# Two-layer decoder step on one core: layer A's y split where it is made, and its transposes moved half a tile back

## The chip, the core and the metric

The kernel runs on one core of a Trainium2 chip. The metric is the device time of one execution in microseconds, as a median over runs. Engines are named as in the trace: PE is TensorE's products, PEld its weight loads, DVE is VectorE, ACT is ScalarE, POOL is GpSimd, and SP is SyncE, whose queue issues the transfers.

## The reference

What is computed, cut to the parts that matter here; D_MODEL is 1024, there are 1024 prompt tokens and 8 x 8 sample tokens, so 1088 rows in all:

```
def short_conv_mixer(u, buf, w_in, w_conv, w_out):        # layer A
    b_gate, c_gate, h, z = split(u @ w_in)
    y, new_buf = causal_dwconv(c_gate * h, buf, w_conv)
    return (b_gate * y * silu(z)) @ w_out, new_buf

def trunk(x, c, ...):
    cs = silu(c)
    for l in range(2):
        shift, scale, gate = split(cs @ w_mod[l] + b_mod[l])
        u = x * (1.0 + scale) + shift
        out = short_conv_mixer(u, ...) if l == 0 else gdn_mixer(u, ...)
        x = layer_norm(ALPHA * x + gate * out, ln_g[l], ln_b[l])
    return x, ...
```

gdn_mixer, layer B, projects u to q, k, v, z and two gate columns for each of 8 heads, convolves, runs a gated delta rule in chunks, norms and projects out.

## The kernel before

Every product is made of three: an operand is split into a high part (a copy rounded to fp32r, on ACT) and a low part (the rest, a subtraction on DVE), and high x high, low x high and high x low are added up in PSUM. The helper split(hi, lo, src) issues the two.

Layer A runs over 8 channel blocks of 128 (chan_a). Each makes four projections of all 1088 tokens, a convolution, and y = b x conv x silu(z), whose last factor POOL multiplies in; y is then stored as fp32 to d_y[0][j]. After the last block comes the out-projection, out_proj(0, ...), over 9 tiles of rows: eight of 128 prompt tokens and tile 8, the 64 samples. For each tile t:

- load_y fetches the tile's y in two halves of four 128-row blocks into a raw buffer and splits it into the parts yh and yl (named wh and wl in the trace). There are three buffers for parts, and one or two for raw data: wts.second lends the second.
- mm(t, hf) does the products of a half: 24 of 512 columns. Tile 8 goes over three column groups instead (512, 256, 256: LAST).
- norm(t) adds the residual x (the tile xt) on DVE, takes the statistics (BN_STATS, BN_AGGR), gets the root from ACT (rt), and computes rs and nm, the scale and bias of the normed tile, in five steps of 128x1.
- finish_a normalizes xt on ACT (xt<-xt,nm,rs). POOL multiplies and adds ln_g and ln_b into x1, which has one buffer and is stored to d_x1. PE transposes the normed tile in eight 128x128 blocks into two PSUM buffers of pt (the trace has t<-cons,xt); below, T0 to T8 are these blocks. ACT applies layer B's modulation (uf, four instructions for each half) and splits it into uh (ACT) and ul (DVE): the operands of layer B's projections.

Behind tile 8, beside_a loads the gate columns (wba) and runs the gate units 0 and 1 (16 products each); gate unit 2 is the first work of gates() in layer B, and needs T8. Layer B's order is written by a planner: streams (chains) and projections (fillers) are taken in the order of times that the class Clock reckons while the program is written. At its start it takes the first step of the chain of gates, and then goes by these times. The order on each engine is what results from the program's order and from the framework's own scheduling; it is fixed before the run.

Of the kernel before, what the change touches and what calls it, by code (L numbers as in the profile page):

```python
# [73 lines left out]
class Clock:  # L74
    """Estimates (in us) of when the queue of an engine gets through what was put into it, and of when tiles are ready;
    they only decide in which order independent work is put into the queues."""

    ready = {}
    # per engine: fixed price, price of an element, from the end until others see the result
# [31 lines left out]
class Weights:  # L111
    """A pool for weight tiles: a buffer for them as loaded (a second one from elsewhere while there is room), buffers for their parts."""
# [18 lines left out]
def tile_trunk(ctx, tc, I, O):  # L131
# [6 lines left out]
    # ------------------------------------------------------------ pools that live throughout  # L138
# [26 lines left out]
    d_y = [dram.tile([KT, P, NT], F32, name=f"d_y{l}") for l in range(2)]  # L165
# [16 lines left out]
    # layer A's prompt shift is kept out of the last group's columns and sits in two columns of its own behind them  # L182
# [7 lines left out]
    def load_half(pool, src, out):  # L190
        """Half of the rows of a weight tile, in two parts; the parts go to out."""
# [53 lines left out]
    def out_proj(l, wk, pairs, wo, gP, gS, finish, ln_in=None, beside=None, constants=None):  # L245
# [14 lines left out]
        def load_y(t, hf):  # L260
            n, o = rows(t)
            yr = wts.raw()
            yh, yl = wts.part()
            SY.dma_start(yr[:, :, :n], d_y[l][4 * hf:4 * hf + 4, :, o:o + n].rearrange("k p t -> p k t"))
            split(yh[:, :, :n], yl[:, :, :n], yr[:, :, :n])
            ys[t, hf] = yh, yl

        def mm(t, hf, cs=(slice(0, 512), slice(512, D))):
            n, o = rows(t)
            if t not in pss:  # L270
                p0, p1 = pair(pairs[t % len(pairs)])
                pss[t] = {0: p0, 512: p1}
                if t == KT:
                    pss[t][768] = bank(0)
# [10 lines left out]
        def norm(t):  # L285
# [4 lines left out]
            cs = (slice(0, 512), slice(512, D)) if t < KT else LAST  # L290
# [21 lines left out]
            return finish(t, n, o, xt, rs, nm, mv[:, 0:1])  # L312
# [11 lines left out]
        else:  # L324
# [5 lines left out]
            load_x(1)  # L330
        wts.second = wk
        stores = []
        for t in range(3, 9):
# [4 lines left out]
            if l and t == 3:  # L338
                for i in EARLY[3]:
                    constants(i) if i < 6 else load_x(i - 6)  # L340
            if t == 3:
                stores.append(norm(0))
            if l:
                load_x(t)
            while stores and t > 3:
                stores.pop(0)()
            stores.append(norm(t - 2))
            if not l:
                load_x(t - 1)
# [9 lines left out]
        if not l:  # L359
            load_x(8)  # L360
            beside()
        stores.append(norm(8))
# [1155 lines left out]
```

## Time and profile before

| | us |
|---|---|
| median of 3 runs | 1397.69 |
| lowest and highest run | 1396.69, 1399.59 |
| span of the profiled execution | 1398.3 |
| layer A, projections | 0 to 430 |
| layer A, out-projection, norm, transposes | 430 to 560 |
| layer B, projections and chunks | 560 to 1290 |
| layer B, out-projection | 1290 to 1398 |

The profiled execution's own time is its span, 1398.3 us; it lies within the runs' range, 0.6 above the median. The bounds of the stages are read off the timeline. A row of the timeline gives start and length in us from the span's start, the engine, the operation with output and inputs, and, in brackets, how long the engine had been idle and which engine, tile or transfer released it. The program's tensors go by their names, t and s and g and o being PSUM tiles.

### The profile page before, as it was taken

The page shows a single profiled execution, that of the slowest core. Times are in us where ns is not written, and L with a number is a line of the kernel's source. Part 1 is how long each engine was busy: PE and PEld are TensorE (multiplying, and loading weights), DVE is VectorE, ACT ScalarE, POOL GpSimd, SP SyncE. Part 2 cuts the span into 40 slices and gives each one's busy share as a digit, 9 for nine tenths or more (in the row PEclk, how much of TensorE's full clock was granted, in tenths as well). Part 3 has the DMA queues.
Part 4 walks back from the last instruction along what each step waited for, and adds up shares of the span by engine and source line. Part 5 has one row for each costly group of instructions (what it writes and reads, how often), then busy time and mean ns, then how long its engine had stood idle before and what let it go on. Part 6 is the DMA issues. An engine that isn't in the chain of part 4 may idle for free.

```text
span 1398.3 us, 27695 instructions
## 1 busy us (share of the span) xinstructions
PE 1325.5 (95%) x10631; PEld 1197.4 (86%) x10631; DVE 907.6 (65%) x2326; ACT 590.8 (42%) x1672; POOL 275.6 (20%) x381
## 2 busy tenths in 40 slices
PE   7999999999999998989999999989999999999897
PEld 5888899999998776988998888988888889887675
DVE  3443234324423988777677988887887887657697
ACT  3421212222111554676656565565555554443221
POOL 0000000000000434112212223231222322221231
PEclk9999999999999999999999999999999999999999
DMA  9735442222213332472121142212222233335862
GB/s 323 246 133 222 163 153 73 72 85 84 68 52 119 121 99 85 152 244 77 32 72 57 50 117 59 87 50 64 74 71 76 75 109 95 115 111 183 241 200 75
DMA packets 119024, 160.23 MB, mean 115 GB/s; under 512 B 21220, under 2 KB 74220, under 8 KB 116844
## 3 DMA queue, kind: packets, MB, share of 16 engines
q1 hardware_dynamic: 118892, 158.46, 35.2%
q8 instruction: 83, 1.36, 0.4%
q14 instruction: 49, 0.40, 0.1%
HBM read 123.61 MB, written 34.82 MB: 113 GB/s over the span
## 4 chain that ended last, share of the span: by engine, by line
PE 33%; DVE 16%; DMA 5%; ACT 4%; issue 2%; POOL 0%; SPq 0%; POOLq 0%; DVEq 0%; ACTq 0%
PE g L106 17%; PE t L106 10%; PE s L106 4%; DVE acc L106 2%; PE o L106 2%; DVE wl L106 2%; DMA wr<-in_wb_dram 1%; ACT junk L106 1%; DMA S<-in_s_dram 1%; DMA rb<-d_rows 1%; DVE EH L106 1%; DVE xt L106 1%; DVE AH L106 1%; DVE YH L106 1%; DVE rk2t L106 1%
## 5 line engine op out<-in xcount | busy, mean ns | idle before, releaser
L106 PE MATMUL g<-uh,wh 128*128 128x384 f32 (+3 forms) x1080 | 381.3, 357 | 3.0 <-ACT xb L106 2.2
L106 PE MATMUL g<-ul,wh 128*128 128x384 f32 (+3 forms) x1080 | 359.9, 336 | 0.0
L106 PE MATMUL g<-uh,wl 128*128 128x384 f32 (+2 forms) x1064 | 356.0, 338 | 0.5 <-DVE wl L106 0.5
L106 DVE TENSOR_TENSOR wl<-wr,wh 128x256 fp32r<-128x256 f32 (+1 forms) x225 | 138.6, 631 | 169.1 <-ACT wh L106 168.7
L106 PEld LDWEIGHTS g<-uh,wh 128*128 128x128 f32 (+1 forms) x1080 | 203.6, 189 | 8.0 <-ACT xb L106 2.7
L106 ACT ACTIVATE wh<-wr 128x256 fp32r<-128x256 f32 (+2 forms) x227 | 108.8, 500 | 236.9 <-PE t L106 117.4
L106 PEld LDWEIGHTS g<-ul,wh 128*128 128x128 f32 (+1 forms) x1080 | 203.7, 189 | 3.3 <-DVE Rs L106 0.2
L106 PEld LDWEIGHTS g<-uh,wl 128*128 128x128 f32 x1064 | 200.9, 189 | 3.8 <-DVE wl L106 1.4
L106 PE MATMUL t<-uh,wh 128*128 128x384 f32 (+3 forms) x540 | 177.2, 336 | 4.6 <-ACT uh L106 3.3
L106 PE MATMUL t<-ul,wh 128*128 128x384 f32 (+3 forms) x540 | 176.3, 334 | 0.1
L106 PE MATMUL t<-uh,wl 128*128 128x384 f32 (+2 forms) x532 | 173.3, 333 | 0.4 <-DVE ve L106 0.4
L106 DVE SCALAR_TENSOR_TENSOR acc<-xb,wbc,acc 128x512 f32<-128x512 f32 (+1 forms) x144 | 118.1, 821 | 10.0 <-ACT acc L106 9.3
L106 PEld LDWEIGHTS t<-uh,wh 128*128 128x128 f32 (+1 forms) x540 | 101.3, 188 | 16.8 <-issue 6.3
L106 PEld LDWEIGHTS t<-ul,wh 128*128 128x128 f32 (+1 forms) x540 | 101.6, 188 | 5.4 <-issue 2.3
L106 PEld LDWEIGHTS t<-uh,wl 128*128 128x128 f32 x532 | 100.2, 189 | 4.0 <-DVE ve L106 0.8
L106 ACT ACTIVATE EH<-t 128x256 f16<-128x256 f32 (+1 forms) x176 | 55.2, 367 | 36.9 <-PE t L106 36.6
L106 ACT ACTIVATE DH<-t 128x256 f16<-128x256 f32 (+1 forms) x128 | 45.8, 383 | 57.6 <-PE t L106 56.8
L106 ACT ACTIVATE xb<-g 128x384 f32<-128x384 f32 (+4 forms) x122 | 48.2, 413 | 37.9 <-PE g L106 36.5
L106 DVE TENSOR_TENSOR YH<-Y,YH 128x256 f16<-128x256 f32 (+1 forms) x104 | 49.5, 479 | 16.8 <-ACT YH L106 16.5
L106 PE MATMUL t<-DH,AH 128*128 128x64 f16 x1176 | 53.5, 193 | 4.1 <-POOL AH L106 1.8
L106 PEld LDWEIGHTS <-AH 128*128 128x128 f16 x1176 | 43.2, 98 | 15.2 <-issue 10.0
L106 PEld LDWEIGHTS <-EH 128*128 128x128 f16 x1120 | 42.7, 98 | 14.5 <-issue 7.6
(367 smaller groups left out, 2432.3 us busy)
## 6 DMA issues: line engine op xcount, KB each, us to landing
wm<-in_wm_dram SPq DMA_DIRECT2D x16, 1024.0 KB
wr<-in_wb_dram SPq DMA_DIRECT2D x64, 256.0 KB
wr<-in_wa_dram SPq DMA_DIRECT2D x62, 256.0 KB
wm<-in_wm_dram SPq DMA_DIRECT2D x16, 512.0 KB
wr<-d_y SPq DMA_DIRECT2D x32, 256.0 KB
S<-in_s_dram SPq DMA_DIRECT2D x32, 256.0 KB
d_y<-cs SPq DMA_DIRECT2D x8, 544.0 KB
wr<-in_wo_dram SPq DMA_DIRECT2D x16, 256.0 KB
```

Source lines behind the costliest of these rows:

```text
L106: return call(*args, **kw)
```

## The change

In chan_a, y is split right after it is complete: the high part into the tile of xb, the low one over sz, and two transfers store them to d_yh and d_yl. load_y of layer A then has two transfers straight into the parts, no raw tile and no split. In out_proj of layer A, norm(t) no longer ends in the transposes: it normalizes, and returns a function that does the rest. That function is called behind the first half of the next tile's products but one (T1 behind all of tile 3's, T6 behind all of tile 8's, T7 and T8 behind the gate units). Tile 8 goes over two groups of 512 columns. gates() gives way once before gate unit 2, until uh[2] and ul[2] are expected. Layer B's out-projection keeps its code. Comments that the change drops aren't shown.

```diff
-    d_y = [dram.tile([KT, P, NT], F32, name=f"d_y{l}") for l in range(2)]
+    d_y = dram.tile([KT, P, NT], F32, name="d_y")
+    d_yh = dram.tile([KT, P, NT], F32, name="d_yh")
+    d_yl = dram.tile([KT, P, NT], F32, name="d_yl")
...
         def load_y(t, hf):
             n, o = rows(t)
-            yr = wts.raw()
-            yh, yl = wts.part()
-            SY.dma_start(yr[:, :, :n], d_y[l][4 * hf:4 * hf + 4, :, o:o + n].rearrange("k p t -> p k t"))
-            split(yh[:, :, :n], yl[:, :, :n], yr[:, :, :n])
-            ys[t, hf] = yh, yl
+            ks = slice(4 * hf, 4 * hf + 4)
+            ys[t, hf] = yh, yl = wts.part()
+            if l:
+                yr = wts.raw()
+                SY.dma_start(yr[:, :, :n], d_y[ks, :, o:o + n].rearrange("k p t -> p k t"))
+                split(yh[:, :, :n], yl[:, :, :n], yr[:, :, :n])
+            else:
+                for x, d in ((yh, d_yh), (yl, d_yl)):
+                    SY.dma_start(x.bitcast(F32)[:, :, :n], d[ks, :, o:o + n].rearrange("k p t -> p k t"))
...
-                if t == KT:
+                if l and t == KT:
                     pss[t][768] = bank(0)
...
-            cs = (slice(0, 512), slice(512, D)) if t < KT else LAST
+            cs = LAST if l and t == KT else (slice(0, 512), slice(512, D))
...
-            return finish(t, n, o, xt, rs, nm, mv[:, 0:1])
+            if l:
+                return finish(t, n, o, xt, rs, nm, mv[:, 0:1])
+            A.activation(xt[:n], xt[:n], AF.Identity, bias=nm[:n], scale=rs)
+            return lambda: finish(t, n, o, xt)
...
-            load_x(1)
-        wts.second = wk
+        if l:
+            wts.second = wk
...
+            while stores and t > 3:
+                stores.pop(0)()
+            if not l:
+                for i in range(2 if t == 3 else 1):
+                    done = norm(t - 3 + i if t == 3 else t - 2)
+                    load_x(t - 2 + i if t == 3 else t - 1)
+                    if t < KT:
+                        mm(t, i)
+                        stores.append(done())
+                    else:
+                        mm(t, 0)
+                        mm(t, 1)
+                        stores.append(done())
+                if 3 < t < KT:
+                    mm(t, 1)
+                continue
...
-        if not l:
+        if l:
+            stores.append(norm(8))
+        else:
             load_x(8)
+            last = [norm(7)]
             beside()
-        stores.append(norm(8))
+            last.append(norm(8))
+            stores += [done() for done in last]
...
             G.tensor_tensor(y, y, sz, ALU.mult)
-            SY.dma_start(d_y[0][j], y)
+            yh, yl = xb[:, :NT].bitcast(F32R), sz.bitcast(F32R)
+            split(yh, yl, y)
+            SY.dma_start(d_yh[j], xb[:, :NT])
+            SY.dma_start(d_yl[j], sz)
...
-        def finish_a(t, n, o, xh, rs, nm, mean):
-            A.activation(xh[:n], xh[:n], AF.Identity, bias=nm[:n], scale=rs)
+        def finish_a(t, n, o, xh):
...
+            yield uh[2], ul[2]
             gate_unit(2)
...
-        next(chains[0][2])
+        chains[0][0] = at(next(chains[0][2])) + SLACK
```

The order shows three places. On PE, where T0 (t_4042 and t_4054 before, t_4077 and t_4089 after) stands among tile 3's products (g<-wo...; a row's products of one weight are two, one for each 512 columns); before:

```order
L106 MATMUL g<-woh_1793,wh 128x512 x2
L106 MATMUL g<-wol_1794,wh 128x512
L106 MATMUL t_4042<-cons,xt 128x128 x4
L106 MATMUL t_4054<-cons,xt 128x128 x4
L106 MATMUL g<-wol_1794,wh 128x512
L106 MATMUL g<-woh_1793,wl 128x512 x2
L106 MATMUL g<-woh_1795,wh 128x512 x2
L106 MATMUL g<-wol_1796,wh 128x512 x2
L106 MATMUL g<-woh_1795,wl 128x512 x2
```

and with the change:

```order
L106 MATMUL g<-woh_1807,wl 128x512 x2
L106 MATMUL g<-woh_1809,wh 128x512 x2
L106 MATMUL g<-wol_1810,wh 128x512 x2
L106 MATMUL g<-woh_1809,wl 128x512 x2
L106 MATMUL t_4077<-cons,xt 128x128 x4
L106 MATMUL t_4089<-cons,xt 128x128 x4
L106 MATMUL g<-woh_1811,wh 128x512 x2
L106 MATMUL g<-wol_1812,wh 128x512 x2
L106 MATMUL g<-woh_1811,wl 128x512 x2
```

T0 moves from the third product pair of tile 3 to the middle of the tile, between its two halves of 24.

On ACT, from the first normed tile on (xt<-xt,nm,rs for tiles 0, 1 and 2; uf<-t is the evacuation of T0 and then T1); before:

```order
L106 ACTIVATE xt<-xt,nm,rs 128x1024
L106 ACTIVATE rt<-ve 128x1
L106 ACTIVATE wh<-wr 128x512
L106 ACTIVATE uf<-t_4042,bp,gp 128x128 x4
L106 ACTIVATE uf<-t_4054,bp,gp 128x128
L106 ACTIVATE uh_98<-uf 128x4x128
L106 ACTIVATE uf<-t_4054,bp,gp 128x128 x3
L106 ACTIVATE uh_98<-uf 128x4x128
L106 ACTIVATE xt<-xt,nm,rs 128x1024
L106 ACTIVATE wh<-wr 128x512
L106 ACTIVATE rt<-ve 128x1
L106 ACTIVATE uf<-t_4092,bp,gp 128x128 x4
```

and with the change:

```order
L106 ACTIVATE xt<-xt,nm,rs 128x1024
L106 ACTIVATE rt<-ve 128x1
L106 ACTIVATE xt<-xt,nm,rs 128x1024
L106 ACTIVATE rt<-ve 128x1
L106 ACTIVATE xt<-xt,nm,rs 128x1024
L106 ACTIVATE uf<-t_4077,bp,gp 128x128 x4
L106 ACTIVATE uf<-t_4089,bp,gp 128x128
L106 ACTIVATE uh_99<-uf 128x4x128
L106 ACTIVATE uf<-t_4089,bp,gp 128x128 x3
L106 ACTIVATE uh_99<-uf 128x4x128
L106 ACTIVATE uf<-t_4153,bp,gp 128x128 x4
```

The normalizing of tiles 1 and 2 moves ahead of the evacuation of T0, and the copies wh<-wr of y are gone.

On ACT at the end of the stage (xt of 128 rows is tile 7, of 64 rows tile 8; wh 128x4x16 is a gate weight, wh 128x256 layer B's first weight, uf<-t_4771 before and t_4709 after the evacuation of T6); before:

```order
L106 ACTIVATE xt<-xt,nm,rs 128x1024
L106 ACTIVATE uf<-t_4771,bp,gp 128x128 x4
L106 ACTIVATE uf<-t_4783,bp,gp 128x128
L106 ACTIVATE uh_100<-uf 128x4x128
L106 ACTIVATE uf<-t_4783,bp,gp 128x128 x3
L106 ACTIVATE wh<-wr 128x4x16
L106 ACTIVATE uh_100<-uf 128x4x128
L106 ACTIVATE rt<-ve 64x1
L106 ACTIVATE xt<-xt,nm,rs 64x1024
L106 ACTIVATE wh<-wr 128x256 x2
L106 ACTIVATE uh_100<-uf 128x4x64 x2
```

and with the change:

```order
L106 ACTIVATE xt<-xt,nm,rs 128x1024
L106 ACTIVATE wh<-wr 128x4x16
L106 ACTIVATE wh<-wr 128x256 x2
L106 ACTIVATE uf<-t_4709,bp,gp 128x128 x4
L106 ACTIVATE uf<-t_4721,bp,gp 128x128
L106 ACTIVATE uh_101<-uf 128x4x128
L106 ACTIVATE uf<-t_4721,bp,gp 128x128 x3
L106 ACTIVATE uh_101<-uf 128x4x128
L106 ACTIVATE rt<-ve 64x1
L106 ACTIVATE xt<-xt,nm,rs 64x1024
L106 ACTIVATE uf<-t_4832,bp,gp 128x128 x4
```

The second gate weight and layer B's first weight move ahead of T6's evacuation. Further on, the order of ACT has 23 table loads (ACT_TABLE_LOAD) where it had 13, the ten new ones between the first gate step and the first chunks of layer B. On PE the last gate unit breaks off after 13 of its 16 products; 48 products of layer B's first unit come next, and then the other three.

## Rows read from the trace of the kernel before

**Rows 1.** Page, part 1: busy us (share of the span) and instructions

```profile
PE 1325.5 (95%) x10631; PEld 1197.4 (86%) x10631; DVE 907.6 (65%) x2326; ACT 590.8 (42%) x1672; POOL 275.6 (20%) x381
```

**Rows 2.** Busy us by stretch: length, PE, PEld, DVE, ACT, POOL; clock, DMA, GB/s

```profile
0.00:430.00 430.00, 422.00 (x2606) 393.65 (x2607) 156.88 (x350) 99.99 (x184) 24.21 (x44) 1.00 0.39 137
...
430.00:560.00 130.00, 120.18 (x574) 94.23 (x573) 97.62 (x167) 57.37 (x123) 48.45 (x31) 0.98 0.35 111
...
475.00:482.00 7.00, 7.00 (x28) 5.57 (x27) 5.63 (x8) 5.11 (x11) 3.87 (x2) 0.76 0.51 187
...
548.00:562.00 14.00, 11.38 (x66) 6.92 (x64) 8.01 (x22) 5.39 (x15) 6.91 (x15) 0.88 0.46 136
...
600.00:620.00 20.00, 17.81 (x112) 17.12 (x111) 13.58 (x43) 16.96 (x37) 1.17 (x4) 1.00 0.68 227
```

**Rows 3.** Waits of TensorE, 430 to 562: us in all, times, the longest

```profile
PE t L106 <- ACT xt L106: 7.2, 5, 2.9
```

**Rows 4.** Timeline of TensorE: start, length, operation, [idle before <-releaser]

```profile
430.39 0.63 PE L106 MATMUL g<-woh,wh 128*128 128x512 f32 x2
...
473.70 1.09 PE L106 MATMUL t<-cons,xt 128*128 128x128 f32 x8 [2.86 <-ACT xt L106]
...
482.33 0.71 PE L106 MATMUL t<-woh,wh 128*128 128x512 f32 x2
...
508.28 1.09 PE L106 MATMUL t<-cons,xt 128*128 128x128 f32 x8 [0.70 <-ACT xt L106]
...
521.28 1.09 PE L106 MATMUL t<-cons,xt 128*128 128x128 f32 x8 [0.71 <-ACT xt L106]
...
548.08 0.34 PE L106 MATMUL g<-uh,wh 128*32 128x384 f32 x1
...
557.22 0.47 PE L106 MATMUL t<-uh,wh 128*32 128x320 f32 x1 [1.77 <-ACT uh L106]
...
561.72 0.44 PE L106 MATMUL g<-uh,wh 128*128 128x384 f32 x1
```

**Rows 5.** Timeline of GpSimd, tiles 0 and 2: the two steps of d_x1

```profile
464.49 2.38 POOL L106 TENSOR_TENSOR x<-xt,ln_g 128x1024 f32<-128x1024 f32 x1 [30.52 <-ACT rt L106]
...
466.95 2.75 POOL L106 TENSOR_TENSOR x<-x,ln_b 128x1024 f32<-128x1024 f32 x1
...
482.37 2.39 POOL L106 TENSOR_TENSOR x<-xt,ln_g 128x1024 f32<-128x1024 f32 x1 [3.43 <-DMA d_x<-x]
```

**Rows 6.** Timeline of VectorE, tiles 0 to 3 and tile 8

```profile
462.88 0.20 DVE L106 TENSOR_SCALAR nm<-mv,rs 128x1 f32<-128x1 f32 x1
...
465.23 2.19 DVE L106 TENSOR_TENSOR wl<-wr,wh 128x512 fp32r<-128x512 f32 x1
...
467.35 2.37 DVE L106 TENSOR_TENSOR rt<-rs,ve 128x1 f32<-128x1 f32 x1
...
479.38 0.21 DVE L106 TENSOR_SCALAR nm<-mv,rs 128x1 f32<-128x1 f32 x1
...
489.83 0.68 DVE L106 SCALAR_TENSOR_TENSOR xt<-xt,tmp 128x512 f32<-128x512 f32 x1
...
553.15 0.20 DVE L106 TENSOR_SCALAR nm<-mv,rs 64x1 f32<-64x1 f32 x1
```

**Rows 7.** Timeline of ScalarE, first a half of y, then tiles 0 and 1

```profile
441.23 0.63 ACT L106 ACTIVATE wh<-wr 128x512 fp32r<-128x512 f32 x1 [7.84 <-DMA wr<-d_y]
...
463.12 1.24 ACT L106 ACTIVATE xt<-xt,nm,rs 128x1024 f32<-128x1024 f32 x1 [4.31 <-DVE nm L106]
...
474.40 1.86 ACT L106 ACTIVATE uf<-t,bp,gp 128x128 f32<-128x128 f32 x5
...
476.65 1.17 ACT L106 ACTIVATE uf<-t,bp,gp 128x128 f32<-128x128 f32 x3
```

**Rows 8.** ScalarE: timeline at 556; group of table loads, 560 to 680

```profile
556.14 0.72 ACT L106 ACTIVATE wh<-wr 128x256 fp32r<-128x256 f32 x2 [1.45 <-DMA wr<-in_wb_dram]
...
L106 ACT ACT_TABLE_LOAD x10 | 12.8, 1283 | 0.8 <-issue 0.7
```

More of the change, by code (lines that the diff above doesn't have):

```diff
@@ L340, in out_proj @@
                     constants(i) if i < 6 else load_x(i - 6)
+            while stores and t > 3:
[14 more added lines that the diff above has]
+                continue
             if t == 3:
                 stores.append(norm(0))
[L343 to L346, printed above, removed]
+            load_x(t)
             stores.append(norm(t - 2))
-            if not l:
-                load_x(t - 1)
             if t < KT:
@@ L358, in out_proj @@
                         mm(t, hf, (c,))
-        if not l:
+        if l:
+            stores.append(norm(8))
+        else:
             load_x(8)
+            last = [norm(7)]
             beside()
-        stores.append(norm(8))
+            last.append(norm(8))
+            stores += [done() for done in last]
         for store in stores:
@@ L822, in gates @@
             V.tensor_scalar(bis, beta, 1.0 / SC, None, ALU.mult)
-            yield 0
+            yield 0.0
             for q0 in range(0, 17, BATCH):
@@ L952, in multiply @@
             G.tensor_tensor(o, o, sz[:, :NT], ALU.mult)
-            SY.dma_start(d_y[1][h], o)
+            SY.dma_start(d_y[h], o)
         def transp(src_list, tg):
@@ L1126, in norm_out @@
                 V.scalar_tensor_tensor(y, ps[:, :nu], nrm, r["vt"], ALU.mult, ALU.mult)
-                store(y, d_y[1])
+                store(y, d_y)
         def scan(h, hf, r):
```

## The prediction

> **What bounds the kernel now.** TensorE is busy for 1325.5 of 1398.3 us [rows 1], so I read the stages one by one and looked in each for what TensorE waits for. In layer A's projections (0 to 430 us) it is never short of work: 422 us busy in the records, while VectorE has 157 and ScalarE 100 of the 430 [rows 2]. In layer A's out-projection (430 to 560) TensorE is busy for 120.2 of 130 us, VectorE for 97.6. The view of waits gives the reason: transposes waited for the normed tile five times, 7.2 us in all, 2.9 the longest [rows 3]. The timeline shows where [rows 4]: 2.86 us before T1 at 473.70, and 0.70 and 0.71 before two later blocks; the remaining two share 2.9. At the end TensorE waits once more, 1.77 us, before the last gate unit at 557.22, and layer B's first product starts at 561.72. The clock falls with the waits: 0.76 granted in 475 to 482 and 0.88 in 548 to 562 [rows 2], which cost some 1.7 us each (7 x 0.24, 14 x 0.12).
>
> From 508.28 to 521.28 a tile takes 13.00 us, whereas its own work is 12.3 (13.00 less the wait of 0.71). So a loop across the other engines sets the pace. Its links: GpSimd multiplies and adds for 2.38 + 2.75 us a tile [rows 5]; while it does, a VectorE instruction that reads two SBUF operands stands still. The split at 465.23 needs 0.69 elsewhere and took 2.19; the 128x1 product at 467.35 took 2.37, where the 128x1 step at 462.88 took 0.20 [rows 6]; they end 0.55 and 0.02 behind a GpSimd instruction (466.87, 469.70). Only then can the next tile's norm end, ScalarE normalize (1.24) and GpSimd start again. It is this loop, and not TensorE's own queue, that I take for the limit.
>
> **The change part by part.** *Splitting y in the channels.* Per channel ScalarE gains a copy of 1088 elements, about 1.3 us by the 1.24 for 1024 [rows 7], and VectorE a subtraction of about 1.4 by 0.68 for 512 [rows 6]. Eight channels add 11 us to each, in a stage where they idle for 270 and more: nothing. The last channel alone stands near a reader. Its y half arrived at 441.23 [rows 7] and is needed at about 447.2 (430.39, the stage's first product [rows 4], plus three halves of 5.6, a tile being 11.2 without its transposes). The two steps and a second write put it back by some 3 us, and its own split, 1.3, is gone: it still comes 4 us early. If that cover is gone it costs at most 3 us. Layer A before 462: 0.
>
> *Eighteen splits out of the out-projection.* 18 ScalarE copies of 0.63 and 18 VectorE subtractions of 0.69 (long ones 2.2) leave. VectorE is the engine in the loop, but after GpSimd's two instructions it still runs two subtractions of the transposed tile, two products, two sums, two statistics at 0.6 each, then about 1.7 of small steps to the next normalizing factor: 1.3 + 5.2 + 4.8 + 1.7 = 13.0 a tile. A subtraction that slips into the gap between GpSimd's two instructions saves 0.6, so 12.4 to 13.0: hardly less than now. What gives TensorE relief is the move: with the transposes half a tile (5.6) later it doesn't meet the loop as long as six tiles lose 0.1 to 0.7 each.
>
> *The start.* In ScalarE's order the normalizing of tiles 1 and 2 now stands ahead of the evacuation of T0. The first factor comes at about 462.0 instead of 462.88, two splits earlier; GpSimd then holds 463.4 to 468.5. Tile 1's 128x1 product waits for that, its factor is there at 469.5 and the tile at 470.8. GpSimd must wait for the store of its one output buffer, 3.43 us [rows 5], so it holds 472 to 477.1, and tile 2's factor, which reaches its product at about 474, comes at 477.6 (479.38 now) [rows 6]; tile 2 is normalized at 478.9. Only then comes T0's evacuation, 1.86 + 0.63 + 1.17 [rows 7]: its second bank is free at about 482.5. TensorE has finished tile 3 at 476.0 (430.39 + 8 halves + T0's 0.85) and wants that bank for T1: a wait of 6.4 us in place of the 2.86. Tile 4 starts at 482.9 (482.33 now), and a wait that is over twice as long leaves the same slow stretch behind it, not now contained in the 482.33, say 1.9: +2.5 us.
>
> The Trainium skill's page "SBUF — State Buffer", section "SBUF: two separate sides", has a rule for this: whichever of the two starts first gets the shared ports for the whole instruction. By it every two-operand VectorE step, however small, pays a GpSimd instruction, as the 2.37 shows; were small ones let through, tile 1's and tile 2's factors would come 2.2 to 3.4 us earlier and the start would cost nothing.
>
> *The loop.* Four waits of 4.3 us (7.2 less 2.9) go: −4.3. So tile 8's products would end 1.8 earlier, and since T6 and T7 (0.85 each: 473.70 to the next product) now stand behind them, at 548.08 − 1.8 − 1.7 = 544.6.
>
> *The tail.* Tile 7's factor comes near 544 (477.6, five tiles of 13.0, 1.4 more in the first of them, where GpSimd again waits for its store), GpSimd holds 545.3 to 550.4, and tile 8's sums wait for that. ScalarE's order now has the second gate weight and the first layer B weight ahead of T6's evacuation. There is one raw buffer; ScalarE waited for such a load until 556.14, 1.45 us past its own work [rows 8], and here the load can't start before the split ahead of it, 545.5 to 548. With 3 us of landing T6's evacuation starts at 548.5 to 551, is done 4.3 later, and tile 8's factor comes at 556 to 557.5 (553.15 now). Then 1.25 for tile 8, 4.3 for T7's evacuation, 1 for tile 8's parts: the last gate unit starts at 562.5 to 564 instead of 557.22. Three of its products and nine small transposes move behind layer B's first 48 products, 1.0 us that is only postponed. Net +4.6 (from +3 to +6.5). TensorE idles there for some 9 us in all instead of 4.3; by the 0.88 of this stretch that costs 0.8 more.
>
> *Layer B's start.* The order has 23 table loads for ScalarE instead of 13, the ten new ones in its first 100 us: 10 x 1.28 = 12.8 us [rows 8]. In 600 to 620 ScalarE is busy for 17.0 of 20 and TensorE for 17.8 [rows 2]; where products wait for a bank that ScalarE empties, a load costs its whole length, else nothing. The gates' small chain comes later and leaves room beside the first products. I take +1, from −3 to +7.
>
> The page "ScalarE: Activation LUTs" of the Trainium skill, section "What ACT_TABLE_LOAD costs", adds a drain and reckons 2.66 us for a switch. By that, ten would be 26.6 us and this term about +2; the ten loads in the rows have 0.8 us of idle time before them in all, so I keep 1.28.
>
> Behind that the order of TensorE is the same as now, so what has gathered by then stays. Into the sum the start and the loop enter only through the tail: they let tile 8's products end 3.5 earlier, but the chain of factors, which sets the tail, doesn't get earlier by that, and the tail's +4.6 is counted against layer B's start itself. Layer A 0, tail 4.6, its slow clock 0.8, layer B's start 1.0: **+6.4 us**. On the profiled 1398.3 that is 1404.7; the median of the runs is 0.6 lower: **1404.1 us**.
>
> **The rivals.** *A: faster.* The two engines exclude each other less than the long rows say once VectorE has 18 subtractions less, and its loop falls under TensorE's 12.3 a tile. Then the start's 2.86 and its slow clock 1.7, and the loop's 4.3, all go, tile 8's products end near 537.5, the last factor comes near 548, and layer B's first product near 555.5: −6, or 1392. For it: VectorE loses 18 splits of 0.7 to 2.2 us in and before this stage. Against it: the loop above closes without a single split. *B: no change.* Small products slip in between GpSimd's instructions in the start (−2.6), a second subtraction slips in per tile, so that the tail begins 4 us sooner, and the late gates cost layer B nothing: −6 on the sum, 1398. *C: slower still.* The ten table loads fall where TensorE waits for ScalarE, and the later gates push back the first chunk chain, of which TensorE waits already; +6 on the sum: 1410. It decides from the point at which ScalarE exceeds some 18 of 20 us in a stretch like 600 to 620. *D: the change does not do what it says:* the splits and the transposes' place were no limit, waits stay 7 us, tail as now, 1398; it shares B's time.
>
> **How the numbers follow.** The measurement tells 0.2%, or 2.8 us, from no change. My forecast (1401 to 1407) has 0.42, C 0.15, A 0.18, B and D 0.25. The forecast and C are slower but for the lowest edge of the first, hence 0.56 slower, 0.25 same, 0.19 faster. The range goes from 1393, most of A, to 1411, C with its bound: about 0.85 is inside by these cases, and its ends are no surer than that.
>
> **What would show it.** Right: after, one wait of about 6 us before T1's second half at 476 to 482, no transposes waiting in tiles 4 to 8, tile 8's products ending within 2 us of 544.6, factors 12.4 to 13 us apart, the last gate unit starting past 562, and 23 table loads. Wrong: factors 12 us apart or less, GpSimd and VectorE's subtractions overlapping, T6's evacuation straight after T6, or a layer B of the same length that starts before 560. If layer B from its first product to the end changes by over 3 us either way, the last term is the one that failed.

## The result, and the profile after

The changed kernel takes 1409.32 us (median; 1408.70 to 1410.37) where the kernel before took 1397.81 beside it: a ratio of 1.0076, 95% interval 1.0052 to 1.0099, so about 11 us or 0.8% slower. The forecast was 1404.1, slower; the time lies inside the range (1393 to 1411), near its upper end.

Three marks divide the loss: the first product of layer A's out-projection, the first product of layer B's projections, and the end. They belong to one core's engines waiting for each other, and repeat: a second profile of the kernel before has 430.59 and 561.92 us for the 430.39 and 561.72 of [rows 4].

| mark, us | before | after | moved by |
|---|---|---|---|
| first product of the out-projection | 430.39 | 434.42 | +4.0 |
| first product of layer B | 561.72 | 568.72 | +7.0 |
| end of the profiled span | 1398.3 | 1406.9 | +8.6 |

So layer A's projections lost 4.0, the out-projection 3.0, and layer B, by these two profiles, 1.6. The page after, part 1 (busy us, share of the span, instructions), against [rows 1]:

```profile
PE 1329.4 (94%) x10607; PEld 1197.9 (85%) x10607; DVE 893.8 (64%) x2314; ACT 600.7 (43%) x1672; POOL 277.8 (20%) x381
```

TensorE is as busy as it was; the time is lost in waiting. The same stretches as in [rows 2], and one more (length, then PE, PEld, DVE, ACT, POOL busy; clock, DMA share, GB/s):

```profile
0.00:430.00 430.00, 418.54 (x2583) 389.77 (x2584) 164.57 (x354) 105.92 (x189) 24.05 (x44) 1.00 0.42 146
...
430.00:560.00 130.00, 121.35 (x555) 94.67 (x553) 75.73 (x143) 43.71 (x94) 47.56 (x29) 0.96 0.48 149
...
548.00:562.00 14.00, 7.02 (x41) 4.15 (x40) 9.31 (x20) 7.70 (x19) 8.28 (x14) 0.84 0.38 121
...
562.00:580.00 18.00, 16.22 (x82) 13.70 (x83) 5.11 (x12) 6.60 (x18) 0.31 (x2) 0.74 0.11 26
```

VectorE went from 97.6 to 75.7 us in 430 to 560 and ScalarE from 57.4 to 43.7: the splits are gone. TensorE's 121.4 are hardly more than its 120.2. The low clock, 0.88 in 548 to 562 before, is now 0.84 there and 0.74 in 562 to 580. In finer windows it is 0.56 and 0.59 in the two halves of 482 to 490, behind the waits before T1, and 0.50, the lower of its two levels (1.2 GHz), from 558 to 571, behind the wait before T8.

The waits of TensorE, 430 to 575 us (us in all, times, the longest), against the 7.2 of [rows 3]:

```profile
PE t L106 <- ACT uf L106: 11.7, 6, 5.2
```

And its timeline at the marks (start, length, operation, [idle before <-releaser]), against [rows 4]:

```profile
434.42 0.63 PE L106 MATMUL g<-woh,wh 128*128 128x512 f32 x2
...
482.97 1.12 PE L106 MATMUL t<-cons,xt 128*128 128x128 f32 x4 [2.71 <-ACT uf L106]
...
484.89 1.11 PE L106 MATMUL t<-cons,xt 128*128 128x128 f32 x4 [0.80 <-ACT uf L106]
...
505.07 1.03 PE L106 MATMUL t<-cons,xt 128*128 128x128 f32 x8
...
517.15 1.03 PE L106 MATMUL t<-cons,xt 128*128 128x128 f32 x8
...
546.88 1.04 PE L106 MATMUL t<-cons,xt 128*128 128x128 f32 x8
...
556.00 0.66 PE L106 MATMUL t<-cons,xt 128*128 128x128 f32 x4 [1.26 <-ACT uf L106]
...
561.84 0.69 PE L106 MATMUL t<-cons,xt 64*128 64x64 f32 x4 [5.18 <-ACT uf L106]
...
564.88 0.47 PE L106 MATMUL t<-uh,wh 128*32 128x320 f32 x1 [0.44 <-ACT uh L106]
...
568.72 0.69 PE L106 MATMUL g<-uh,wh 128*128 128x384 f32 x1
```

The loop's waits are gone: between 484.89 and tile 8's last product TensorE never waits for a transpose, and its tiles are 12.08 us apart (505.07, 517.15) instead of 13.00. In their place it waits at the start, 2.71 + 0.80 before T1, and at the end, 1.26 before T7's second half and 5.18 and more before T8; the last gate unit starts at 564.88 instead of 557.22.

Layer A lost most of its 4 us in two like places, for channels 1 and 2. ScalarE's timeline at the first:

```profile
134.40 1.11 ACT L106 ACTIVATE xb<-cs 128x1088 fp32r<-128x1088 f32 x1 [3.17 <-POOL cs L106]
...
135.41 0.58 ACT L106 ACTIVATE part<-s 128x512 f32<-128x512 f32 x1
```

TensorE's at the same place:

```profile
136.04 0.66 PE L106 MATMUL o<-cons,part 128*128 128x128 f32 x4 [1.62 <-ACT part L106]
```

The copy of y into its high part (xb<-cs) waits for GpSimd's product, idle for 3.17 us; behind it stands the evacuation of a modulation product (part<-s), which needs nothing of y, and TensorE waits 1.62 us for that. The second place, at 196, costs 1.65.

VectorE in the loop and at tile 8, against [rows 6]; nm<-mv,rs is a tile's factor, ul<-uf,uh the two halves of the transposed tile before it:

```profile
498.65 0.80 DVE L106 TENSOR_TENSOR ul<-uf,uh 128x512 fp32r<-128x512 f32 x1 [3.62 <-ACT uh L106]
...
500.36 1.89 DVE L106 TENSOR_TENSOR ul<-uf,uh 128x512 fp32r<-128x512 f32 x1 [0.91 <-ACT uh L106]
...
507.33 0.21 DVE L106 TENSOR_SCALAR nm<-mv,rs 128x1 f32<-128x1 f32 x1
...
519.83 0.21 DVE L106 TENSOR_SCALAR nm<-mv,rs 128x1 f32<-128x1 f32 x1
...
558.88 0.20 DVE L106 TENSOR_SCALAR nm<-mv,rs 64x1 f32<-64x1 f32 x1
```

From factor to factor it is 12.50 us, more than TensorE's 12.08: the factors fall behind by 0.4 us a tile, and the half tile of slack takes that up. Within the 12.50, VectorE stands idle for 3.62 us until ScalarE has evacuated the first half, and the second half's subtraction takes 1.89 in GpSimd's shadow, which means that it ends 0.55 us behind a GpSimd instruction beside it (498.98 to 501.70) where it takes 0.68 alone.

### The profile page after: what moved, and what is told of

Read it like the earlier page. It is cut to its first block, busy times and chain, and to the rows that moved or that the text cites. A ratio compares the mean times of both kernels' runs of the same rounds, so it can differ in the third digit from the quotient of the medians.

```text
span 1406.9 us, 27637 instructions
## 1 busy us (share of the span) xinstructions
PE 1329.4 (94%) x10607; PEld 1197.9 (85%) x10607; DVE 893.8 (64%) x2314; ACT 600.7 (43%) x1672; POOL 277.8 (20%) x381
## 4 chain that ended last, share of the span: by engine, by line
PE 32%; DVE 17%; DMA 5%; ACT 4%; issue 2%; POOL 1%; SPq 0%; POOLq 0%; ACTq 0%; DVEq 0%
PE g L106 17%; PE t L106 10%; PE s L106 4%; DVE acc L106 3%; PE o L106 2%; DVE wl L106 2%; ACT junk L106 1%; DMA rb<-d_rows 1%; DVE EH L106 1%; DVE YH L106 1%; DVE xt L106 1%; DVE rb L106 1%; DMA ln_b<-in_ln_b_dram 1%; DVE f1t L106 1%; DVE AH L106 1%
## 5 line engine op out<-in xcount | busy, mean ns | idle before, releaser
L106 DVE TENSOR_TENSOR wl<-wr,wh 128x256 fp32r<-128x256 f32 (+1 forms) x207 | 114.4, 568 | 143.6 <-ACT wh L106 143.3
L106 ACT ACTIVATE wh<-wr 128x256 fp32r<-128x256 f32 (+1 forms) x209 | 97.6, 491 | 204.6 <-PE t L106 111.6
```

What stands on the lines that cost most here:

```text
L106: return call(*args, **kw)
```

## The experiments

All kernels were profiled and, but for the last, timed against the kernel before in rounds. Two profiles of one kernel agree in the marks to 0.2 us, and kernels with the same layer A to 0.7 (434.40 to 435.14); the total, which scatters over 6 to 13 us in these runs, is given as a ratio to the kernel before, run beside it.

| kernel | ratio, 95% interval | out-projection starts | factors of tiles 7, 8 | layer B starts |
|---|---|---|---|---|
| before | 1 | 430.39 | 542.70, 553.15 | 561.72 |
| after | 1.0076, 1.0052 to 1.0099 | 434.42 | 544.83, 558.88 | 568.72 |
| split at the source alone | 0.9967, 0.9948 to 0.9985 | 435.14 | 539.10, 549.55 | 556.89 |
| the order alone | 1.0049, 1.0029 to 1.0068 | 430.72 | 545.94, 556.77 | 566.62 |
| after, copy on GpSimd | 1.0047, 1.0031 to 1.0062 | 432.89 | 543.40, 557.33 | 567.18 |
| after, old gates' start | 1.0069, 1.0045 to 1.0093 | 434.58 | 545.05, 558.99 | 569.56 |
| split alone, copy put later | 0.9952, 0.9935 to 0.9969 | 430.23 | 534.18, 544.63 | 553.76 |
| after, no ln_b on GpSimd | 0.9997, 0.9979 to 1.0016 | 435.05 | 535.31, 549.74 | 559.58 |
| after, second raw buffer | 1.0057, 1.0034 to 1.0080 | 434.40 | 544.91, 556.80 | 566.65 |
| split, moved in the loop only | 1.0004, 0.9983 to 1.0025 | 434.99 | 544.62, 555.08 | 562.49 |
| after, copy put later | 1.0044, 1.0028 to 1.0059 | 431.08 | 541.48, 555.40 | 565.25 |
| before, a second profile | not timed | 430.59 | 542.83, 553.27 | 561.92 |

**The two halves apart.** The first kernel is the one before with y split at its source and nothing moved:

```diff
             G.tensor_tensor(y, y, sz, ALU.mult)
-            SY.dma_start(d_y[0][j], y)
+            yh, yl = xb[:, :NT].bitcast(F32R), sz.bitcast(F32R)
+            split(yh, yl, y)
+            SY.dma_start(d_yh[j], xb[:, :NT])
+            SY.dma_start(d_yl[j], sz)
```

and load_y as in the change. Expected:

> The kernel before with only one half of the change: y is split in the channels, stored as two tensors and loaded straight into the parts; the transposes, tile 8's column groups and the gates keep their old places. Theory (the split's copy on ScalarE stands ahead of the evacuation of a modulation product and makes TensorE wait twice in layer A; the pace of the out-projection is set by the factors' chain with GpSimd, which needs no split of y): the stage's first product comes 4 us later than the 430.39 of before, the out-projection stays within 2 us of its length (waits of transposes 4 to 8 us), layer B the same: 1400 to 1404. Rival (the removed splits free the out-projection, the moved transposes spoil it): waits of transposes under 2 us, out-projection 5 us shorter, total at or below before: 1393 to 1398.

TensorE's waits up to 575 us, the stretch of the tail, TensorE's two marks, and VectorE in the loop:

```profile
PE o L106 <- ACT part L106: 4.8, 3, 1.6
...
PE t L106 <- ACT xt L106: 2.0, 3, 0.8
```

```profile
548.00:562.00 14.00, 12.37 (x77) 9.00 (x76) 7.58 (x32) 6.73 (x14) 3.07 (x14) 1.00 0.36 100
```

```profile
435.14 0.63 PE L106 MATMUL g<-woh,wh 128*128 128x512 f32 x2
...
556.89 0.44 PE L106 MATMUL g<-uh,wh 128*128 128x384 f32 x1
```

```profile
493.43 0.68 DVE L106 TENSOR_TENSOR ul<-uf,uh 128x512 fp32r<-128x512 f32 x1
...
495.72 1.29 DVE L106 TENSOR_TENSOR tmp<-t,gateP 128x512 f32<-128x512 f32 x2 [0.71 <-PE t L106]
...
496.93 5.28 DVE L106 SCALAR_TENSOR_TENSOR xt<-xt,tmp 128x512 f32<-128x512 f32 x2
...
505.73 0.21 DVE L106 TENSOR_SCALAR nm<-mv,rs 128x1 f32<-128x1 f32 x1
...
516.70 0.21 DVE L106 TENSOR_SCALAR nm<-mv,rs 128x1 f32<-128x1 f32 x1
```

The theory held for layer A (+4.75; 4.8 us of waiting for part, of which 0.9 stood before) and fell for the out-projection. That is 121.75 us long, from 435.14 to 556.89, where it was 131.33: the removed splits are worth 9.6 us, and the kernel is faster than before by 0.3%. Part of the 9.6 is the clock, which is 1.00 from 430 to 560 here: the last gate unit's 16 products take 2.9 us (553.54 to 556.40) where they took 4.0 (557.22 to 561.23). The factors come 10.97 us apart, not 12.4 to 13. That is less than TensorE's own 12.08 a tile (508.52, 520.60, 532.68), so here the factors catch up, and TensorE sets the pace. In this order VectorE has the next tile's products with the gate (tmp, which read PSUM) and its sums (xt) right behind a factor. The products run at full speed while GpSimd works (a tile later 0.69 and 0.68, at 508.49 and 509.10, beside GpSimd's 507.41 to 509.79), the two sums share its shadow (5.28 for both, until 502.21, beside GpSimd's 496.48 to 501.66), and the subtractions ul follow when ScalarE has long been done: 0.68 each and no idle time.

The second kernel has the moved transposes and gates but one d_y, raw tiles and splits in the out-projection, with the second raw buffer:

```diff
-            yh, yl = xb[:, :NT].bitcast(F32R), sz.bitcast(F32R)
-            split(yh, yl, y)
-            SY.dma_start(d_yh[j], xb[:, :NT])
-            SY.dma_start(d_yl[j], sz)
+            SY.dma_start(d_y[0][j], y)
...
-        if l:
-            wts.second = wk
+        wts.second = wk
```

> The changed kernel with the other half undone: y is stored once as fp32 and loaded and split in the out-projection as before; the moved transposes, the two column groups of tile 8 and the later gates stay. Theory: layer A is as before (first product of the stage at 430.4), the start's and the tail's waits remain (layer B's first product 4 to 9 us later than the 561.72 of before), and layer B keeps its 23 table loads: 1402 to 1408. Rival (all of the loss comes from splitting y at its source): 1396 to 1399, layer B's first product within 1 us of before.

```profile
430.72 0.63 PE L106 MATMUL g<-woh,wh 128*128 128x512 f32 x2
...
559.74 0.69 PE L106 MATMUL t<-cons,xt 64*128 64x64 f32 x4 [6.03 <-ACT uf L106]
...
566.62 0.69 PE L106 MATMUL g<-uh,wh 128*128 128x384 f32 x1
```

The theory holds for layer A and the tail: layer B starts 4.9 us later, with a wait of 6.03 before T8, the longest of nine that make 13.5 us, and the kernel is 0.5% slower in all. At the start only 0.34 us of waiting before T1 are left. The order alone loses, the split alone gains, and together they lose more than the sum of both (−0.3% and +0.5%, measured +0.8%). That isn't quite like for like, as the order alone has the second raw buffer and the kernel after has not. With that buffer (below) the kernel after is at +0.6% and its out-projection at 132.25 us, against the 135.90 of the order alone: of the split's 9.6 us there, 3.65 are left in the new order.

**Where the move costs.** The split at the source, with the old start, tail and gates, and only the transposes of tiles 2 to 5 half a tile later:

```diff
-            stores.append(norm(t - 2))
+            half = not l and 3 < t < KT
+            later = norm(t - 2, half)
+            if not half:
+                stores.append(later)
...
                 for hf in range(2):
                     mm(t, hf)
+                    if half and hf == 0:
+                        stores.append(later())
```

> The split of y at its source with the transposes moved half a tile only in the loop of tiles 4 to 7; the start, the tail with tile 8's three column groups, and the gates are as before. Theory (the move puts normalizing ahead of the evacuation in ScalarE's queue, so the factors come 12.5 us apart instead of 11, and the tail starts that much later): tile 7's factor 3 to 6 us later than the 539.1 of the split alone, layer B's first product 3 to 6 us later than its 556.9. Rival (the start and the tail alone carry the loss of the move, 12 us in all): factors 11 to 11.5 us apart, layer B's first product within 1.5 us of the split alone.

VectorE and TensorE:

```profile
506.36 0.22 DVE L106 TENSOR_SCALAR nm<-mv,rs 128x1 f32<-128x1 f32 x1
...
510.20 0.79 DVE L106 TENSOR_TENSOR ul<-uf,uh 128x512 fp32r<-128x512 f32 x1 [3.62 <-ACT uh L106]
...
511.91 1.87 DVE L106 TENSOR_TENSOR ul<-uf,uh 128x512 fp32r<-128x512 f32 x1 [0.92 <-ACT uh L106]
...
518.86 0.21 DVE L106 TENSOR_SCALAR nm<-mv,rs 128x1 f32<-128x1 f32 x1
```

```profile
534.34 0.73 PE L106 MATMUL t<-cons,xt 128*128 128x128 f32 x4 [3.40 <-ACT uf L106]
...
562.49 0.44 PE L106 MATMUL g<-uh,wh 128*128 128x384 f32 x1
```

The theory holds. The factors are 12.50 us apart again, with the same 3.62 of idle time and 1.87 for the 1.89 of the kernel after; layer B starts 5.6 later than with the split alone, and T6, which stands near the tail, waits 3.40. In ScalarE's order tile t's normalizing now precedes the evacuation of T(t−1), and in VectorE's order the subtractions ul of that evacuation precede the next tile's products. So each factor waits for 1.24 of normalizing, 1.84 and 0.65 of evacuation, and only then for VectorE's own work, with one subtraction in GpSimd's shadow. That the evacuation could go first without loss wasn't tried.

Next the changed kernel without the addition of ln_b (x1 then lacks it):

```diff
                 G.tensor_tensor(x1, xh, lnv[0], ALU.mult)
-                G.tensor_tensor(x1, x1, lnv[1], ALU.add)
```

> The changed kernel without GpSimd's addition of ln_b in layer A's norm, so that GpSimd works 2.4 us a tile in place of 5.1; the x that layer B's norm takes is short of ln_b by that. Theory of the prediction (GpSimd's two instructions hold up VectorE, and this sets the pace of the factors): from factor to factor 10 to 11.5 us in the loop instead of 12.5, tile 7's factor 3 us or more earlier than 544.8, layer B's first product 4 to 8 us earlier than 568.7. Rival (after the change it is ScalarE's queue that sets the pace: normalizing stands ahead of the evacuation of the tile before, and VectorE idles 3.6 us for it in each tile): factors 11.5 to 12.5 us apart, tile 7's factor less than 3 us earlier, layer B's first product 0 to 3 us earlier.

```profile
500.60 0.21 DVE L106 TENSOR_SCALAR nm<-mv,rs 128x1 f32<-128x1 f32 x1
...
504.43 0.78 DVE L106 TENSOR_TENSOR ul<-uf,uh 128x512 fp32r<-128x512 f32 x1 [3.62 <-ACT uh L106]
...
506.15 0.69 DVE L106 TENSOR_TENSOR ul<-uf,uh 128x512 fp32r<-128x512 f32 x1 [0.93 <-ACT uh L106]
...
511.92 0.21 DVE L106 TENSOR_SCALAR nm<-mv,rs 128x1 f32<-128x1 f32 x1
```

By the numbers set out the prediction's theory holds and the rival falls: 11.32 us apart, where the one wanted 10 to 11.5 and the other 11.5 to 12.5, tile 7's factor 9.5 earlier, and layer B's 9.1 even past the 4 to 8. By the rows it is neither alone. The second subtraction falls from 1.89 to 0.69, which is the 1.2 that the interval loses; the 3.62 of idle time stay, so ScalarE's part of the loop is as large as before. The start gains too (tile 2's factor at 476.51 instead of 480.04, though its stage began 0.6 later), and the loop takes 6.0 us less up to tile 7's factor. In the tail nothing is gained: tile 8's sums no longer wait for GpSimd but for TensorE's products (VectorE idle for 1.84 us until 541.32), and tile 8's factor follows tile 7's after 14.43 us instead of 14.05. GpSimd's shadow is worth as much as all of the loss (ratio 0.9997), in the start and the loop.

**The tail's raw buffer.** The changed kernel with wts.second = wk for layer A too, as in the second kernel:

> The changed kernel with the second raw buffer that the kernel before had from tile 3 on, so that the gate weights and layer B's first weight need not wait for one buffer. Theory (the load of layer B's first weight holds up the evacuation of T6 until 552.5, and with it tile 8's statistics): T6's evacuation starts at 547 to 549, tile 8's factor comes 1.5 to 3 us earlier than 558.9, layer B's first product the same. Rival (GpSimd's last tile holds VectorE until 551.4 anyway): tile 8's factor within 1 us of 558.9 and no change of the total.

ScalarE's evacuation of T6, here and in the kernel after, where layer B's first weight (wh<-wr 128x256) comes first:

```profile
548.72 1.84 ACT L106 ACTIVATE uf<-t,bp,gp 128x128 f32<-128x128 f32 x5
```

```profile
551.92 0.72 ACT L106 ACTIVATE wh<-wr 128x256 fp32r<-128x256 f32 x2 [5.40 <-DMA wr<-in_wb_dram]
...
552.55 1.84 ACT L106 ACTIVATE uf<-t,bp,gp 128x128 f32<-128x128 f32 x5
```

T6's evacuation starts at 548.72 in place of 552.55, tile 8's factor and layer B's first product come 2.1 earlier, as the theory has it; GpSimd's last tile sets the rest (tile 8's two sums take 4.22 us and end 0.55 behind its last instruction, 551.78). The ratio, 1.0057, can't be told from 1.0076.

**Layer A's two waits.** The changed kernel with the copy on GpSimd:

```diff
-            split(yh, yl, y)
+            G.tensor_copy(yh, y)
+            V.tensor_tensor(yl, y, yh.bitcast(F32), ALU.subtract)
```

> The changed kernel with the high part of y copied by GpSimd, which has just made y, in place of ScalarE; nothing else. Theory (ScalarE's copy waits for GpSimd's product with a modulation product's evacuation queued behind it): the two waits of TensorE for part, 1.62 and 1.65 us, go, the stage's first product comes at 430.5 to 431 in place of 434.42, and all that follows comes as much earlier, since the chain of factors starts with the first tile: 1405 to 1406 against 1409.3. Rival (the out-projection's chain ends where it does whatever comes before): layer A is shorter but layer B's first product stays at 568 to 569, total 1408 to 1410.

```profile
196.55 0.45 PE L106 MATMUL o<-part,sel 128*64 128x512 f32 x1 [1.26 <-DVE xg L106]
...
432.89 0.63 PE L106 MATMUL g<-woh,wh 128*128 128x512 f32 x2
```

ScalarE's two waits go, but one comes back on VectorE: its subtraction now waits for GpSimd with the addition of a gate's bias (xg) queued behind, and TensorE waits 1.26 for that. Layer A is 1.5 shorter instead of 4, and layer B's start follows by the same 1.5, so the rival falls.

Put later, for channels 1 and 2, with a zero made from the next channel's first product as the copy's bias; first with the split alone:

```diff
+                if late:
+                    zero = aw.tile([P, 1], F32, name="zero")
+                    V.tensor_scalar(zero, bias[:, 0:1], 0.0, None, ALU.mult)
+                    late.pop(0)(zero)
...
+            def store_y(zero):
+                A.activation(yh, y, AF.Identity, bias=zero)
+                V.tensor_tensor(yl, y, yh.bitcast(F32), ALU.subtract)
```

> The split of y at its source with the transposes in their old places, and for channels 1 and 2 the copy on ScalarE tied to a value of the next channel's first product, so that it stands behind the evacuation of the modulation product. Theory (in layer A only the place of the copy in ScalarE's queue costs): the two waits of 1.6 us for part go, the stage's first product comes at 430.5 to 432 in place of 435.1, layer B's first product at 552 to 554 in place of 556.9, and the total falls by 3 to 5 us against the split alone: 1392 to 1394 by the ratio to before (0.992 to 0.994). Rival (the two transfers and VectorE's subtraction cost layer A as much): the first product stays at 434 to 435, total as with the split alone.

```profile
430.23 0.63 PE L106 MATMUL g<-woh,wh 128*128 128x512 f32 x2
...
553.76 0.44 PE L106 MATMUL g<-uh,wh 128*128 128x384 f32 x1
```

The stage starts at 430.23: the whole of layer A's loss was the copy's place in the queue. Layer B starts 8.0 us earlier than in the kernel before, and the kernel is 0.5% faster than that (0.9952, 0.9935 to 0.9969), the lowest ratio here. Against the split alone the ratio fell by 0.0015, where 3 to 5 us were expected, and the two intervals overlap: the totals don't tell these two kernels apart, the marks do. Of the 4.9 us that the start of the stage won, 3.1 arrive at layer B's first product; 1.4 are lost in the last gate unit, which runs at a granted clock of 0.61 (550.76 to 553.76) and takes 4.3 us where it took 2.9 at 1.00.

Then the same edit in the changed kernel:

> The changed kernel whole, with the copy of y for channels 1 and 2 tied behind the modulation product's evacuation, as in the late split. Theory (the wait in layer A and the loss by the moved transposes are two separate terms, and the chain of factors starts with the stage's first product): the first product at 430 to 431 in place of 434.4, tile 7's factor 4 us earlier than 544.8, layer B's first product 4 us earlier than 568.7; by the ratio to before 0.3% better than the changed kernel's 1.0069 to 1.0076. Rival (the tail ends where it does): layer B's first product within 1.5 us of 568.7.

The stage starts at 431.08, tile 7's factor comes at 541.48 and layer B's first product at 565.25: 3.3, 3.4 and 3.5 earlier. The two terms stand apart and add. With its layer A nearly mended, the changed kernel is still 0.44% or 6.2 us slower than the kernel before.

**The gates.** The changed kernel with the gates' start of before:

```diff
-            yield uh[2], ul[2]
             gate_unit(2)
...
-        chains[0][0] = at(next(chains[0][2])) + SLACK
+        next(chains[0][2])
```

> The changed kernel with the gates' start as before: no step given way before gate unit 2, and the first step of the chain of gates taken at once; 13 table loads in place of 23. Theory (the later gates and their ten table loads cost layer B about 1.5 us, from 568.72 to the end 838.2 against 836.6 before): 1407 to 1408.5 against 1409.3. Rival (table loads lie beside other work and cost nothing, and the 48 products ahead of the rest of the gate unit even hide its wait): 1409 to 1411. A second rival (the later gates are the larger part of the loss): 1402 to 1405.

The ratio is 1.0069 with 13 table loads and 1.0076 with 23: no difference that can be told. Layer B's first product is 0.8 later, since the gate unit's last three products and the small transposes are ahead of it again. Neither theory is told from the other; the second rival, that the gates are the larger part of the loss, is out.

**How far one profile goes.** The kernel before, again:

> The kernel before, profiled a second time, to see what one profile can tell apart. Expected: the stage's first product within 0.5 us of 430.39, layer B's first product within 0.5 us of 561.72, as the same waits stand on one core's engines; layer B, where many transfers run, may differ by some us from its 836.6.

The marks came as expected, at 430.59 and 561.92, within 0.2 us. The span is 1393.8 instead of 1398.3: all of 4.5 us of scatter lies in layer B. So the 1.6 us that layer B seemed to lose can't be read from two profiles.

## Why the prediction was right, and where not

The direction and the range held. The sum held less well: a layer A that was thought free, a tail that was sized too high, and a rest behind layer B's first product that was sized too low or isn't told from scatter.

- *Layer A, 0.* Wrong by 4.0, and the step that failed is the argument from idle time: ScalarE was idle for 330 of 430 us, yet it takes its queue in order, and the copy's wait for GpSimd stood ahead of an evacuation that TensorE needed. The margin that was checked, the last channel's y, was indeed ample: TensorE waits for no part of y in the out-projection. Shown by the late split, with and without the move.
- *Eighteen splits, "hardly less than now".* The number 12.4 to 13.0 came true (12.50), its reason only in half. In the old order the same removal takes the factors from 13.0 (tiles 4 and 5) to 10.97 and the stage from 131.3 to 121.75 us, so that the loop "closes without a single split" was wrong for that order. What kept them at 12.5 is the new order, in which evacuation and subtraction of the tile before come ahead of the next tile's sums. The prediction had GpSimd's 5.2 as the link before VectorE's subtractions; the rows show ScalarE's 3.8 there, with 1.2 of GpSimd's shadow.
- *The start, +2.5.* Tile 2's factor came at 480.04; the 477.6 of the prediction with layer A's 4.0 is 481.6. TensorE stood at T1 for 3.5 us and not 6.4. As forecast, the factor waited for GpSimd's second instruction, but that ended at 479.99, 1.1 sooner than the 477.1 and 4.0 of the forecast, and the factor came right behind it instead of 0.5 later. T1's first half ran before its second half's bank was free, 1.1 us that the forecast counted as waiting. So tile 4 started at 485.66; less layer A's 4.0 that is 0.7 earlier than before, where 0.6 later was forecast. But the slow stretch, 0.56 and 0.59 in 482 to 490, is 3.4 us by the prediction's way of reckoning, where it took 1.9.
- *The loop, −4.3.* Right: no wait from tile 4 to tile 8. Tile 8's products ended at 546.88, 1.7 before the 544.6 + 4.0 of the forecast.
- *The tail, +4.6, and 0.8 for the clock.* With the 4.0 of layer A, tile 8's factor should have come at 560 to 561.5 and the last gate unit at 566.5 to 568; they came at 558.88 and 564.88. The 5.4 us up to layer B's first product stand against 3.0 measured. The mechanism is right: factors 12.5 a tile, GpSimd's last tile, and the first weight ahead of T6, of which the second raw buffer gave back 2.1. The sizes were off both ways: tile 7's factor came 3.2 before its 544 + 4.0, 1.6 of it by the start and 1.6 in the five tiles (64.8 us for 66.4), and tile 8's followed after 14.05 in place of 12 to 13.5. TensorE's waits in the tail came to 8.6 us, near the 9 forecast, with a clock of 0.50 behind the longest, where the 0.8 was reckoned with 0.88. And 4.6 isn't the middle of the prediction's own links: 562.5 to 564 against 557.22, less 1.0, are 4.3 to 5.8.
- *Layer B, +1, and 1.0 put off.* Not settled. The kernels with the new tail lie 1 to 4 us further from before by their ratio than by their mark, those with the old tail within 1.5; 1.0 of that are the three products and transposes. In the kernel after, some 1.1 more are the clock, an estimate from the rows of TensorE: layer B's products come 0.32 us apart from 569.21 to 571.13 and 0.17 apart from 571.53 on. Table loads show no cost.
- *The time from the span.* The prediction took 0.6 off, because the profiled span, 1398.3, lies above the median. That step was wrong: in each of the profiled runs here the time is 1.8 to 2.4 us longer than the span (after, 1409.14 for 1406.9), so the profile of before, at some 1398.3 + 2.0, stood some 2.5 above the middle of its runs, and its layer B was 4.7 longer than in the second profile. By the medians the change costs 11.5, by the two spans 8.6.
- *The rivals.* A and B took it that less work on VectorE would speed up the loop. That holds for the split alone, which is faster than before, and not for the changed kernel. C, table loads that TensorE waits for, isn't borne out. D isn't either: the loop's waits did go, and others came.

Of the signs named for "right", the factors, the loop without waits and the 23 table loads came. The wait at T1 was 3.5 and not about 6, tile 8's products ended 2.3 past 544.6, and the last gate unit, at 564.88, started past 562 only by layer A's 4.0.

The direction was right, by the tail. That the time lay 5 us above the forecast is a sum of three misses: layer A 4.0 more, the out-projection 2.4 less (3.0 for 5.4), and by the medians 3.5 more behind layer B's first product (4.5 for 1.0). That they left it inside the range is in part luck. The changed kernel with the late copy, 6.2 us above before by its ratio, is the case that the forecast of +6.4 described; there too the sum fits better than its terms, 0.7, 2.8 and 2.7 for 0, 5.4 and 1.0.

## What to carry to other kernels

Idle time of an engine says nothing about a wait that is put into the middle of its queue: ask what stands behind it and who needs that, here one copy ahead of one evacuation, twice 1.6 us. When a change takes work away and moves other work at once, build both halves: here one is worth 0.3%, and by its marks some 3 us more with its two waits mended, while both together lose 0.8%. And a consumer that is put off half a tile so that TensorE needn't wait also puts off its own followers: the slack that TensorE won was paid back at the end of the stage, where nothing lies beside it.

## What the runs showed of the hardware

ScalarE's table load before the first root ran ahead of need in the kernel before (453.22, the root at 457.64). With the splits gone it waited with the root:

```profile
460.97 1.28 ACT L106 ACT_TABLE_LOAD   x1 [21.89 <-DVE ve L106]
...
462.27 0.20 ACT L106 ACTIVATE rt<-ve 128x1 f32<-128x1 f32 x1
```

It starts when VectorE's value is there, after 21.89 us of idle time, and puts its 1.28 us in front of the root, in the kernel after and with the split alone, not with the order alone (453.55, the root at 457.97). Why the wait stands at the load in the one and at the root in the other, no run here shows.

The exclusion of VectorE and GpSimd is not one block for a pair of GpSimd instructions. VectorE and GpSimd at tile 2's factor in the kernel after:

```profile
476.90 0.63 DVE L106 TENSOR_TENSOR rt<-rs,ve 128x1 f32<-128x1 f32 x1
...
477.57 0.16 DVE L106 SCALAR_TENSOR_TENSOR rt<-rt,rs 128x1 f32<-128x1 f32 x1
```

```profile
475.01 2.51 POOL L106 TENSOR_TENSOR x<-xt,ln_g 128x1024 f32<-128x1024 f32 x1 [2.88 <-DMA d_x<-x]
...
477.60 2.39 POOL L106 TENSOR_TENSOR x<-x,ln_b 128x1024 f32<-128x1024 f32 x1
```

A 128x1 step that meets a running GpSimd instruction ends when that one ends, 477.53 for 477.52, so it pays only what is left of it. The next step starts in the gap of 0.08 us and takes its usual 0.16. The one behind it, at 477.76, meets the second instruction and takes 2.24, until 480.00 for 479.99. The step at 467.46 took 2.22 in the same way (469.68 for 469.66). The Trainium skill's page "SBUF — State Buffer", section "SBUF: two separate sides", gives the lock for the whole of one instruction, and these rows agree with that.
